# Split activations and weights in other places of SBUF: block pitches of 1040, 1056, 1072 and 2080 bytes in a hybrid mLSTM and gated-delta block

## The chip, the cores and the metric

The kernel runs on one core of one Trainium2 chip. The metric is the device time of one execution in microseconds (us); the time before is the median of three runs.

## What is computed

One layer of a bidirectional encoder block in float32, with 256 tokens of width 2048, and a final norm:

```python
mod = silu(c) @ W_ada + b_ada                    # shift, scale, gate for both sub-layers
h = rms_norm(x) * (1 + scale_m) + shift_m
proj = h @ w_in                                  # q, k, v, gates of two branches, merge gates
y_a = (sigmoid(a_o) * norm(bidirectional mLSTM)) @ w_branch_a
y_b = (norm(bidirectional gated delta rule) * silu(b_z)) @ w_branch_b
x = x + gate_m * ((g_a * y_a + g_b * y_b) @ w_out)
hf = rms_norm(x) * (1 + scale_f) + shift_f
gt, up = split(hf @ w_gate_up)                   # 2048 -> 2 x 5632
x = x + gate_f * ((silu(gt) * up) @ w_down)      # 5632 -> 2048
return rms_norm(x)
```

## The kernel before

Almost all of the work is large matrix products of the 256 tokens with weights that come once from HBM. For more precision than one pass of the fast float32 form (`float32r`) gives, each operand is split in a high part (a copy rounded to that form, made by ScalarE) and a low part (the remainder, a subtraction on VectorE). A product is then three matmuls: high x high, low x high, high x low.

The activations are kept split, transposed, in blocks of 128 features: a tile `[128, 16 blocks, 256 tokens]` of 16 KB in each partition, one for the high and one for the low part. `big` makes these for the mixer: `hh`/`hl` (the normed input), `obh`/`obl` and `hah`/`hal` (the outputs of the two branches), `mgh`/`mgl` (their merge). `hfh`/`hfl` (the normed input of the feed-forward part, 16 blocks) and `ffh`/`ffl` (its inner activation, 44 blocks) are made at their place (lines 876 to 879).

Weights are split as they arrive, in two kinds of job:

- `tjob` gives 256 tokens x 512 columns. A chunk of 1 MB (four blocks of 128 x 512) is loaded into `raw` by a DMA from the SP queue. For each pair of blocks ScalarE writes `wh` (line 153) and VectorE `wl` (line 154), and twelve matmuls follow: per block and token half the lines 159, 160 and 161. The **stationary** operand is a 128 x 128 piece of the activations, `xh` or `xl`; the **moving** one is a block of 512 columns of `wh` or `wl`. There are 32 such jobs of four chunks in the mixer (`z`, `v`, `o`, `ma`, `mb` on `hh`/`hl`, four each, `yb`, `ya` and the output projection, named `o` too in the profile, but with `mgh`/`mgl`), 22 in the feed-forward part (`gt`, `up`), and 4 of eleven chunks (`d`): 6240 matmuls.
- `fjob` gives 128 features x 256 tokens (names `b` and `a` in the profile, lines 135 to 137): there the weights are the stationary operand and `hh`/`hl` the moving one, with 256 columns. There are 49 such jobs: 2352 matmuls.

`raw`, `wh` and `wl` have three buffers each, which both kinds of job share; so each of `wh` and `wl` has three slots of 4 KB, and a slot holds two blocks of a `tjob`.

Until about 1175 us the jobs run as filling between the steps of the two recurrent branches and of the modulation vectors (`ada`, VectorE), in an order written out by hand. Then come `yb`, `ya`, the output projection, from about 1468 us on `gt` and `up` in turn, and from about 1966 us `d`, one job after the other.

The places of these tiles in a partition, before the change, in bytes:

| tile | start | modulo 128 | pitch of its blocks |
|---|---|---|---|
| `wh`, three slots | 46880, 50976, 55072 | 32 | 2048 (`tjob`), 512 (`fjob`) |
| `wl`, three slots | 59168, 63264, 67360 | 32 | 2048, 512 |
| `hh`, `hl` | 196576, 212960 | 96 | 1024 |
| `obh`, `obl` and later `mgl`, `mgh` | 79680, 96064 | 64 | 1024 |
| `hah`, `hal` | 196576, 212960 | 96 | 1024 |
| `hfh`, `hfl` | 169760, 186144 | 32 | 1024 |
| `ffh`, `ffl` | 71456, 116512 | 32 | 1024 |

The second half of the tokens lies 512 bytes behind the first, so it has the same remainder modulo 128.

Of the kernel before, what the change touches and what calls it, by code (L numbers as in the profile page):

```python
# [10 lines left out]
F32R = mybir.dt.float32r  # L11
# [4 lines left out]
P = 128  # L16
T = 256
D = 2048
KB = D // P
# [4 lines left out]
FB = FF // P  # L24
# [26 lines left out]
def hybrid_block(ctx: ExitStack, tc: tile.TileContext, xr, nfr, crow, pk_d, cst_d, ada2, ada4, win0, winb, wint, wba, wbb, wo, wgu, wd, out, dbg=None):  # L51
# [3 lines left out]
    def pool(stack, name, bufs=1, **kw):  # L55
        return stack.enter_context(tc.tile_pool(name=name, bufs=bufs, **kw))

    cp = pool(ctx, "cp")
    st = pool(ctx, "st")
# [4 lines left out]
    bigA = pool(sa, "bigA", 2, side="right")  # L64

    def big(p, dt, name):
        return p.tile([P, KB, T], dt, tag="b16", name=name)

    def gps(name):
        return g_ps.tile([P, 512], F32, tag="g", name=name)  # L70
# [45 lines left out]
    def pump():  # L116
        count[0] += 1
        if background and count[0] % 2 == 0:
            if next(background[0], None) is None:
                background.pop(0)  # L120
# [22 lines left out]
    def tjob(name, chunks, xh, xl, done):  # L143

        ps = [acc_ps.tile([P, 512], F32, tag="acc", name=f"acc_{name}_{t}") for t in range(2)]
        last = 4 * len(chunks) - 1
        for u, src in enumerate(chunks):
            raw = st.tile([P, 4, 512], F32, tag="raw", bufs=3, name=f"raw_{name}_{u}")
            nc.sync.dma_start(raw, src)
            for k0 in range(0, 4, 2):  # L150
                wh = st.tile([P, 2, 512], F32R, tag="wh", bufs=3, name=f"wh_{name}_{u}_{k0}")
                wl = st.tile([P, 2, 512], F32R, tag="wl", bufs=3, name=f"wl_{name}_{u}_{k0}")
                S.activation(wh, raw[:, k0 : k0 + 2], AF.Copy)  # L153
                V.tensor_tensor(wl, raw[:, k0 : k0 + 2], wh.bitcast(F32), ALU.subtract)  # L154
                for k in range(2):
                    kk = 4 * u + k0 + k
                    for t in range(2):
                        c = slice(t * P, (t + 1) * P)
                        PE.matmul(ps[t], xh[:, kk, c], wh[:, k], start=kk == 0, stop=False)  # L159
                        PE.matmul(ps[t], xl[:, kk, c], wh[:, k], start=False, stop=False)  # L160
                        PE.matmul(ps[t], xh[:, kk, c], wl[:, k], start=False, stop=kk == last)  # L161
                if k0:
                    pump()
                    if u == len(chunks) - 1:
                        done(ps)
                yield True
# [32 lines left out]
    inv_d = [tc.dram_tile([64, 32, 32], F32, name=f"inv_d{g}") for g in range(NH_B // GRP)]  # L199

    hh = big(bigA, F32R, "hh")
    hl = big(bigA, F32R, "hl")

    evp = pool(sa, "evp", side="right")
# [31 lines left out]
    with ExitStack() as s0:  # L236
# [24 lines left out]
        for b in range(KB):  # L261
# [6 lines left out]
            for i in range(2):  # L268
                f = 1.0 if i else pk[:, PK_NMIX + b : PK_NMIX + b + 1]
# [21 lines left out]
        u = w0.tile([P, T], F32, name="u")  # L291
# [275 lines left out]
    def z_job(g):  # L567
        def done(ps):
            szs[g] = evp.tile([P, 2, 512], F32, tag="sz", bufs=1, name=f"sz{g}")
            for t in range(2):  # L570
                S.activation(szs[g][:, t], ps[t], AF.Silu)
        return tjob(f"z{g}", [wint[g, u] for u in range(4)], hh, hl, done)
# [7 lines left out]
    def a_vo(i, h):  # L580
        return tjob(
            f"{'vo'[i]}{h}", [wint[4 + 4 * i + h, u] for u in range(4)], hh, hl,
            keep((v_d, o_d)[i][h], (AF.Copy, AF.Sigmoid)[i], f"{'vo'[i]}{h}"),
        )

    def m_job(i, g):
        return tjob(
            f"m{'ab'[i]}{g}", [wint[12 + 4 * i + g, u] for u in range(4)], hh, hl,
            keep((ma_d, mb_d)[i][g], AF.Sigmoid, f"m{'ab'[i]}{g}"),
        )  # L590
# [82 lines left out]
    bigC = pool(sc, "bigC", 2)  # L673
    ml = pool(sm_, "ml")
    obh, obl = big(bigC, F32R, "obh"), big(bigC, F32R, "obl")

    def o_split(g):
# [195 lines left out]
    fp = pool(ctx, "fp")  # L873
    sh = ExitStack()
    hp = pool(sh, "hp", side="right")
    hfh = hp.tile([P, KB, T], F32R, name="hfh")
    hfl = hp.tile([P, KB, T], F32R, name="hfl")
    ffh = fp.tile([P, FB, T], F32R, name="ffh")
    ffl = fp.tile([P, FB, T], F32R, name="ffl")
    for q in range(4):  # L880
        xn = hp.tile([P, 2, 512], F32, tag="sg", bufs=2, name=f"xn{q}")
        for t in range(2):
# [1 line left out]
        for e2 in range(2):  # L884
            px = gps(f"pxn{q}_{e2}")
            hf = hp.tile([P, 2, T], F32, tag="hf", bufs=1, name=f"hf{q}_{e2}")
            for e in range(2):
                f = 2 * e2 + e
# [14 lines left out]
    for j in range(FB // 4):  # L903
# [5 lines left out]
        for e2 in range(2):  # L909
            px = gps(f"pxf{j}_{e2}")  # L910
            for e in range(2):
                f = 2 * e2 + e
# [119 lines left out]
```

## Time and profile before

| | |
|---|---|
| median of 3 runs | 2219.57 us (2217.16 to 2230.97) |
| the profiled execution | 2226.21 us, span 2224.4 us |
| granted TensorE clock in it | 0.979 |
| TensorE busy | 2096.3 us (94%) |
| VectorE busy | 1408.9 us (63%) |
| ScalarE busy | 994.9 us (45%) |
| DMA | 485.83 MB, mean 218 GB/s |

PE is TensorE, PEld its loading of stationary operands, DVE is VectorE, ACT ScalarE, POOL GpSimd, SP SyncE. A group of instructions is shown by line, engine and operation, then out<-in by the names of the tiles with shapes and xcount; behind the first bar stand its busy time in us and the mean of one in ns, behind the second the engine's idle time before it and what ended that. A row of the timeline has its start in us, its length in us, engine, line, operation and tiles. A row of the windows has the stretch, its length, and for each engine its busy time with the number of its instructions; then the granted clock as a share, the share of DMA time and GB/s. Matmuls are pipelined and their ends are modelled, so their lengths overlap.

### The profile page before, as it was taken

The page shows a single profiled execution, that of the slowest core. Times are in us where ns is not written, and L with a number is a line of the kernel's source. Part 1 is how long each engine was busy: PE and PEld are TensorE (multiplying, and loading weights), DVE is VectorE, ACT ScalarE, POOL GpSimd, SP SyncE. Part 2 cuts the span into 40 slices and gives each one's busy share as a digit, 9 for nine tenths or more (in the row PEclk, how much of TensorE's full clock was granted, in tenths as well). Part 3 has the DMA queues.
Part 4 walks back from the last instruction along what each step waited for, and adds up shares of the span by engine and source line. Part 5 has one row for each costly group of instructions (what it writes and reads, how often), then busy time and mean ns, then how long its engine had stood idle before and what let it go on. Part 6 is the DMA issues. An engine that isn't in the chain of part 4 may idle for free.

```text
span 2224.4 us, 27756 instructions
## 1 busy us (share of the span) xinstructions
PE 2096.3 (94%) x10756; PEld 1754.7 (79%) x10756; DVE 1408.9 (63%) x2120; ACT 994.9 (45%) x1399; POOL 103.6 (5%) x206
## 2 busy tenths in 40 slices
PE   5989989998998899989999999989999999999997
PEld 4867778978887888778787787868888888878886
DVE  4677777886788677845557776564544454454454
ACT  3146436644564456434443444444444444444443
POOL 0002101100210111010000000000000000000000
PEclk9999999999999999999999999999999999999999
DMA  8976665675667455756787676545555555555553
GB/s 308 416 303 194 184 215 187 204 248 191 192 236 241 163 189 205 255 201 231 286 318 269 241 291 232 186 141 191 190 183 191 191 190 183 192 199 189 192 197 122
DMA packets 82645, 485.83 MB, mean 218 GB/s; under 512 B 10681, under 2 KB 21057, under 8 KB 28113
## 3 DMA queue, kind: packets, MB, share of 16 engines
q1 hardware_dynamic: 68672, 459.34, 58.0%
q0 software_dynamic: 6496, 9.49, 2.7%
q10 hardware_dynamic: 7346, 15.24, 1.8%
q8 instruction: 84, 1.38, 0.2%
q14 instruction: 47, 0.39, 0.0%
HBM read 467.21 MB, written 16.82 MB: 218 GB/s over the span
## 4 chain that ended last, share of the span: by engine, by line
PE 60%; DVE 4%; DMA 3%; issue 2%; ACT 1%; POOL 0%; DVEq 0%; ACTq 0%; POOLq 0%
PE acc_gt L159 4%; PE acc_gt L160 4%; PE acc_up L161 4%; PE acc_up L160 4%; PE acc_up L159 4%; PE acc_d L160 4%; PE acc_gt L161 4%; PE acc_d L159 4%; PE acc_d L161 4%; PE acc_o L160 2%; PE acc_o L161 2%; PE acc_o L159 2%; DMA ada<-ada 1%; PE acc_ya L160 1%; PE acc_ya L159 1%
## 5 line engine op out<-in xcount | busy, mean ns | idle before, releaser
L154 DVE TENSOR_TENSOR wl_up<-raw_up,wh_up 128x1024 fp32r<-128x1024 f32 x88 | 107.9, 1226 | 128.7 <-ACT wh_up L153 128.7
L154 DVE TENSOR_TENSOR wl_d<-raw_d,wh_d 128x1024 fp32r<-128x1024 f32 x88 | 107.8, 1226 | 123.2 <-ACT wh_d L153 123.2
L154 DVE TENSOR_TENSOR wl_gt<-raw_gt,wh_gt 128x1024 fp32r<-128x1024 f32 x88 | 107.8, 1225 | 109.3 <-ACT wh_gt L153 109.3
L107 DVE SCALAR_TENSOR_TENSOR ada<-ada,crow 128x2048 f32<-128x2048 f32 x64 | 146.2, 2284 | 39.2 <-DMA ada<-ada 39.2
L135 PE MATMUL acc_b<-hh,wh_b 128*128 128x256 f32 x576 | 167.3, 290 | 0.0
L137 PE MATMUL acc_b<-hh,wl_b 128*128 128x256 f32 x576 | 162.5, 282 | 1.1 <-DVE wl_b L132 1.1
L136 PE MATMUL acc_b<-hl,wh_b 128*128 128x256 f32 x576 | 162.9, 283 | 0.0
L153 ACT ACTIVATE wh_d<-raw_d 128x1024 fp32r<-128x1024 f32 x88 | 93.3, 1061 | 138.9 <-PE acc_d L160 132.0
L153 ACT ACTIVATE wh_gt<-raw_gt 128x1024 fp32r<-128x1024 f32 x88 | 93.3, 1060 | 133.9 <-PE acc_gt L160 78.9
L153 ACT ACTIVATE wh_up<-raw_up 128x1024 fp32r<-128x1024 f32 x88 | 93.2, 1060 | 117.8 <-PE acc_up L160 84.6
L159 PE MATMUL acc_gt<-wh_gt,hfh 128*128 128x512 f32 x352 | 138.8, 397 | 1.3 <-ACT hfh L183 1.1
L160 PE MATMUL acc_gt<-wh_gt,hfl 128*128 128x512 f32 x352 | 139.4, 396 | 0.0
L161 PE MATMUL acc_gt<-wl_gt,hfh 128*128 128x512 f32 x352 | 138.7, 394 | 0.0
L159 PE MATMUL acc_d<-wh_d,ffh 128*128 128x512 f32 x352 | 137.4, 390 | 0.0
L160 PE MATMUL acc_d<-wh_d,ffl 128*128 128x512 f32 x352 | 137.4, 390 | 0.0
L161 PE MATMUL acc_d<-wl_d,ffh 128*128 128x512 f32 x352 | 137.0, 389 | 0.0
L161 PE MATMUL acc_up<-wl_up,hfh 128*128 128x512 f32 x352 | 136.9, 389 | 0.0
L159 PE MATMUL acc_up<-wh_up,hfh 128*128 128x512 f32 x352 | 136.9, 389 | 0.0
L160 PE MATMUL acc_up<-wh_up,hfl 128*128 128x512 f32 x352 | 136.9, 389 | 0.0
L274 PE MATMUL first<-x,raw 128*128 128x256 f32 x512 | 111.6, 380 | 2.0 <-ACT x L271 2.0
L135 PEld LDWEIGHTS acc_b<-hh,wh_b 128*128 128x128 f32 x576 | 110.6, 192 | 2.1 <-issue 1.4
L137 PEld LDWEIGHTS acc_b<-hh,wl_b 128*128 128x128 f32 x576 | 110.8, 192 | 1.7 <-DVE wl_b L132 1.7
(339 smaller groups left out, 5375.8 us busy)
## 6 DMA issues: line engine op xcount, KB each, us to landing
ada<-ada SPq DMA_DIRECT2D x64, 1024.0 KB, 5.4
raw_gt<-wgu SPq DMA_DIRECT2D x44, 1024.0 KB, 4.9
raw_up<-wgu SPq DMA_DIRECT2D x44, 1024.0 KB, 4.9
raw_d<-wd SPq DMA_DIRECT2D x44, 1024.0 KB, 4.8
raw_b<-winb SPq DMA_DIRECT2D x36, 1024.0 KB, 5.4
ra<-ada SPq DMA_DIRECT2D x32, 1025.0 KB, 12.7
raw<-win SPq DMA_DIRECT2D x16, 1024.0 KB, 10.5
raw_z<-wint SPq DMA_DIRECT2D x16, 1024.0 KB, 5.8
```

The lines of the kernel that those rows point to most:

```text
L107: V.scalar_tensor_tensor(raw, raw, 1.0, row_c[:, :D], ALU.mult, ALU.mult, accum_out=mod[:, c0 + b : c0 + b + 1])
L135: PE.matmul(o, wh[:, k], hh[:, kk], start=kk == 0, stop=False)
L136: PE.matmul(o, wh[:, k], hl[:, kk], start=False, stop=False)
L137: PE.matmul(o, wl[:, k], hh[:, kk], start=False, stop=kk == KB - 1)
L153: S.activation(wh, raw[:, k0 : k0 + 2], AF.Copy)
L154: V.tensor_tensor(wl, raw[:, k0 : k0 + 2], wh.bitcast(F32), ALU.subtract)
L159: PE.matmul(ps[t], xh[:, kk, c], wh[:, k], start=kk == 0, stop=False)
L160: PE.matmul(ps[t], xl[:, kk, c], wh[:, k], start=False, stop=False)
L161: PE.matmul(ps[t], xh[:, kk, c], wl[:, k], start=False, stop=kk == last)
L274: PE.matmul(first[o], raw[:, o], x[:, b], start=b == 0 and o % 2 == 0, stop=b == KB - 1 and o % 2 == 1)
```

## The change

The tiles that hold split operands are made a little longer in their last dimension, and only the old part of each is used. `big` allocates 260 instead of 256 tokens (16 bytes more a block, 16640 instead of 16384 bytes a tile), `wh` and `wl` of `tjob` 520 instead of 512 columns (32 bytes; the slots, which `fjob` shares, grow from 4096 to 4160 bytes), `hfh`/`hfl` 264 tokens (32 bytes), `ffh`/`ffl` 268 tokens (48 bytes). Everything allocated behind them moves by the difference: on the left side by 6 x 64 = 384 bytes, on the right by 512. Order, engines, operations and shapes of the instructions stay as they are; operands that spread over several blocks have a step between the blocks.

```diff
     def big(p, dt, name):
-        return p.tile([P, KB, T], dt, tag="b16", name=name)
+        return p.tile([P, KB, T + 4], dt, tag="b16", name=name)[:, :, :T]
...
             for k0 in range(0, 4, 2):
-                wh = st.tile([P, 2, 512], F32R, tag="wh", bufs=3, name=f"wh_{name}_{u}_{k0}")
-                wl = st.tile([P, 2, 512], F32R, tag="wl", bufs=3, name=f"wl_{name}_{u}_{k0}")
+                wh = st.tile([P, 2, 520], F32R, tag="wh", bufs=3, name=f"wh_{name}_{u}_{k0}")[:, :, :512]
+                wl = st.tile([P, 2, 520], F32R, tag="wl", bufs=3, name=f"wl_{name}_{u}_{k0}")[:, :, :512]
...
-    hfh = hp.tile([P, KB, T], F32R, name="hfh")
-    hfl = hp.tile([P, KB, T], F32R, name="hfl")
-    ffh = fp.tile([P, FB, T], F32R, name="ffh")
-    ffl = fp.tile([P, FB, T], F32R, name="ffl")
+    hfh = hp.tile([P, KB, T + 8], F32R, name="hfh")[:, :, :T]
+    hfl = hp.tile([P, KB, T + 8], F32R, name="hfl")[:, :, :T]
+    ffh = fp.tile([P, FB, T + 12], F32R, name="ffh")[:, :, :T]
+    ffl = fp.tile([P, FB, T + 12], F32R, name="ffl")[:, :, :T]
```

## The prediction

> **What bounds the kernel now.** I read the page's engine totals first, then three windows of the span, then the groups of the last stage.
>
> ```profile
> PE 2096.3 (94%) x10756; PEld 1754.7 (79%) x10756; DVE 1408.9 (63%) x2120; ACT 994.9 (45%) x1399; POOL 103.6 (5%) x206
> ...
> PE 60%; DVE 4%; DMA 3%; issue 2%; ACT 1%; POOL 0%; DVEq 0%; ACTq 0%; POOLq 0%
> ...
> L154 DVE TENSOR_TENSOR wl_d<-raw_d,wh_d 128x1024 fp32r<-128x1024 f32 x88 | 107.8, 1226 | 123.2 <-ACT wh_d L153 123.2
> ...
> L153 ACT ACTIVATE wh_d<-raw_d 128x1024 fp32r<-128x1024 f32 x88 | 93.3, 1061 | 138.9 <-PE acc_d L160 132.0
> ...
> L159 PE MATMUL acc_d<-wh_d,ffh 128*128 128x512 f32 x352 | 137.4, 390 | 0.0
> ```
>
> ```profile
> core 0: us, PE busy (x) PEld busy (x) DVE busy (x) ACT busy (x) POOL busy (x), PEclk, DMA share, GB/s
> 0.00:1175.00 1175.00, 1068.44 (x6222) 921.20 (x6222) 833.73 (x1513) 558.01 (x909) 103.63 (x206) 0.97 0.68 236
> 1175.00:1460.00 285.00, 283.62 (x1235) 225.30 (x1236) 188.44 (x222) 119.86 (x148) 0.00 (x0) 0.99 0.68 243
> 1460.00:2225.00 765.00, 744.24 (x3301) 608.24 (x3299) 386.73 (x387) 317.08 (x342) 0.00 (x0) 0.99 0.54 182
> ```
>
> TensorE has work in 94% of the span. Behind 1175 us it hardly stops: ScalarE waits for TensorE (L153 <-PE), VectorE for ScalarE, TensorE for nobody (0.0 idle before L159). There a split pair costs ScalarE 1.061 and VectorE 1.226 us, while its 12 matmuls take 12 x 0.2267 = 2.72 us, so both have slack. The 390 ns "mean" of a matmul is a modelled length that overlaps the next one. What counts is the distance from start to start, which I take from the timeline: first and last row of a stretch without a gap, over the number of steps between.
>
> In the d stage (stationary ffh/ffl, both 32 past a multiple of 128, as the moving wh/wl are), 178 rows:
>
> ```profile
> 1999.82 0.39 PE L160 MATMUL acc_d<-wh_d,ffl 128*128 128x512 f32 x1
> ...
> 2039.94 0.39 PE L160 MATMUL acc_d<-wh_d,ffl 128*128 128x512 f32 x1
> ```
>
> 40.12 / 177 = 0.2267 us. In the o stage (stationary mgh/mgl, 64 past a multiple of 128), 173 rows:
>
> ```profile
> 1399.72 0.40 PE L161 MATMUL acc_o<-wl_o,mgh 128*128 128x512 f32 x1
> ...
> 1439.85 0.40 PE L159 MATMUL acc_o<-wh_o,mgh 128*128 128x512 f32 x1
> ```
>
> 40.13 / 172 = 0.2333 us. The windows of both (us, TensorE busy and its matmuls, granted clock, DMA share, GB/s) show a full clock:
>
> ```profile
> 1400.00:1440.00 40.00, 40.00 (x173) 1.00 0.56 188
> 1980.00:2200.00 220.00, 220.00 (x973) 1.00 0.55 186
> ```
>
> The instructions have the same line and shape; what differs is where the stationary blocks lie. With hh/hl (96 past a multiple of 128) there are two values, over 37 and 36 rows:
>
> ```profile
> 249.71 0.39 PE L161 MATMUL acc_v<-wl_v,hh 128*128 128x512 f32 x1
> ...
> 257.95 0.39 PE L161 MATMUL acc_v<-wl_v,hh 128*128 128x512 f32 x1
> ...
> 689.71 0.40 PE L160 MATMUL acc_z<-wh_z,hl 128*128 128x512 f32 x1
> ...
> 697.88 0.40 PE L159 MATMUL acc_o<-wh_o,hh 128*128 128x512 f32 x1
> ```
>
> 8.24 / 36 = 0.2289 and 8.17 / 35 = 0.2334 us: the same places give either, so the rhythm locks into one of several states. How it settles is to be seen in the feed-forward stage behind a break:
>
> ```profile
> 1522.21 0.39 PE L160 MATMUL acc_gt<-wh_gt,hfl 128*128 128x512 f32 x1
> 1522.44 0.40 PE L161 MATMUL acc_gt<-wl_gt,hfh 128*128 128x512 f32 x1
> 1522.67 0.39 PE L159 MATMUL acc_gt<-wh_gt,hfh 128*128 128x512 f32 x1
> 1522.90 0.40 PE L160 MATMUL acc_gt<-wh_gt,hfl 128*128 128x512 f32 x1
> 1523.13 0.39 PE L161 MATMUL acc_gt<-wl_gt,hfh 128*128 128x512 f32 x1
> 1523.37 0.39 PE L159 MATMUL acc_gt<-wh_gt,hfh 128*128 128x512 f32 x1
> ```
>
> Five steps take 1.16 us, 0.232 each, before it falls to 0.2267. So a rhythm that isn't locked costs about 0.232, and the best lock is that of places with equal remainders, which is what the feed-forward stages have.
>
> At half clock the excess is gone. The window 685 to 688 us, then its first and last of eight rows:
>
> ```profile
> 685.00:688.00 3.00, 3.00 (x8) 0.50 0.49 126
> ...
> 685.05 0.63 PE L160 MATMUL acc_z<-wh_z,hl 128*128 128x512 f32 x1
> ...
> 688.04 0.63 PE L161 MATMUL acc_z<-wl_z,hh 128*128 128x512 f32 x1
> ```
>
> 2.99 / 7 = 0.427, half of which is 0.2136: the floor that a full-clock matmul would have without the excess of 0.013 to 0.020 us.
>
> **The change part by part.** No instruction is added, removed or moved. The start of every block of the split operands changes, and the 6240 matmuls of 512 columns read both operands from them. Pitches become 1040 bytes for hh/hl and all other 16-block activations, 1056 for hfh/hfl, 1072 for ffh/ffl, 2080 between the two halves of wh/wl. Modulo 128 the moving operand then begins at 32 or 96 (first half) and at 0 or 64 (second half); the stationary one steps by 16, 32 or 48 from block to block. The equal remainders of the feed-forward stages are given up: this is the change's cost.
>
> (1) gt and up, 2112 matmuls. The stationary blocks step by 32, so differences from the moving operand are multiples of 32. The rows give 0.2267 for 0, 0.2289 for 64, 0.2333 for 32 (64 against 32); I take 0.2333 for 96 too, mean 0.2306. 2112 x 0.0039 = +8.2 us. Bounds: 0, if each matmul finds the best lock, and 2112 x 0.0066 = +13.9, if each has the worst.
>
> (2) d, 1056 matmuls, steps of 48, each pair with another difference: I take the unlocked 0.232, +5.6 us; bounds 0 and +7.0.
>
> (3) Jobs on hh/hl (z, v, o, ma, mb), 1920 matmuls, steps of 16: now between 0.2289 and 0.2334, middle 0.2312; afterwards 0.232: +1.5 us, bounds -8.6 (all at 0.2267) and +8.4 (0.2289 to 0.2333).
>
> (4) ya, 384 matmuls, whose hah/hal lie as hh/hl do, from 0.2289: +1.2 us. yb and the output projection, 768, from 0.2333: -1.0. Together between -5.9 and +1.7.
>
> (5) The feature-major jobs, 2352 matmuls of 256 columns. Here hh is the moving operand. Two rhythms, 18 and 15 rows:
>
> ```profile
> 835.95 0.28 PE L137 MATMUL acc_b<-hh,wl_b 128*128 128x256 f32 x1
> ...
> 837.88 0.28 PE L136 MATMUL acc_b<-hl,wh_b 128*128 128x256 f32 x1
> ...
> 832.94 0.28 PE L136 MATMUL acc_b<-hl,wh_b 128*128 128x256 f32 x1
> ...
> 834.59 0.28 PE L135 MATMUL acc_b<-hh,wh_b 128*128 128x256 f32 x1
> ```
>
> 1.93 / 17 = 0.1135 and 1.65 / 14 = 0.1179. Both states are there already; I take 0, bounds -5 and +5 (half the difference x 2352).
>
> (6) ScalarE and VectorE write wh, wl and the split activations in pieces with a gap between. Places off a multiple of 16 bytes are read already: the convolution's four taps begin 0, 4, 12 and 16 bytes into a padded row.
>
> ```profile
> L233 DVE SCALAR_TENSOR_TENSOR cv<-pad,pk,cv x192: 440/479/490, 146.7 to 874.1; 128x256 f32<-128x256 f32 x192
> ```
>
> Minimum, median and maximum over the 192 lie within 50 ns, so a start costs VectorE next to nothing. I take 0. If each split grew by 50 ns, the 2.29 us of a pair stay below 2.72 and are hidden behind the matmuls. Without that cover, in the first 1175 us, the 274 splits there (20 jobs of 8, 49 of 2, 16 blocks of hh) x 0.05 = +14 us at worst.
>
> Sum: 8.2 + 5.6 + 1.5 + 1.2 - 1.0 = +15.5 us. The profiled execution took 2226.2 (span 2224.4 and 1.8 around it), so it would come to 2241.7; it lies 6.6 above the median shown, 2219.6, and against that median the forecast is 2235.
>
> **The rivals.**
>
> Faster: the excess over 0.2136 comes from a start that is off by 32 modulo 64. Every moving block that the rows show begins so, and none of these matmuls reaches the floor; that speaks for it as far as it goes. Afterwards the second halves of wh/wl begin at multiples of 64. If these 3120 matmuls fall from 0.2267 to 0.2136, that is -41 us, and the other half pays half of my sum, +8: 2187. Against it: only the stationary place differs between 0.2267 and 0.2333, so the excess is at least partly a meeting of the two reads.
>
> Slower still: differences of an odd multiple of 16, which no row shows, cost a further step as large as from 0.2267 to 0.2333, so 0.24. This touches half of d and half of the jobs on hh, ya, yb and o: 2064 x 0.008 = 16.5. The 1176 feature-major matmuls with such a moving block pay 0.0066 as well, 7.8. With my sum, +40: 2260. For it: each smaller unit of misplacement in the rows (64, then 32) costs more. Against it: 32 against 64 could be the worst case.
>
> No change: the difference between the stages has another cause than the remainders, or blocks that begin at multiples of 16 are all alike. Then 2220. By the Trainium skill, SBUF — State Buffer, section "Specifications (TRN2)", a line is 16 bytes long, and by its "Who interferes with whom" TensorE's two read ports are independent and TensorE waits for no one; all starts here stay on such lines, so by that rule the change moves nothing. The rows of one line and shape at 0.2267 and 0.2333 speak against that reading of the rule. Nor does the kernel become another program: VectorE, ScalarE and the queues keep order and sizes.
>
> **How the numbers follow.** The places in steps (1) and (2) leave a lock that only equal remainders show, and I see no way to keep it: 50 in 100 for the forecast, 2235 with its own range 2222 to 2252. Faster 22 in 100 (2187), slower still 18 (2260), no change 10 (2220). A measurement of this kernel can tell about 1% from no change, 22 us: 2197 and 2242. Of the forecast's 50, 20 lie beyond 2242, since the bounds of (1) to (4) add up to +31. So faster by over 1% is 0.22, within 1% 0.30 + 0.10 = 0.40, slower 0.20 + 0.18 = 0.38. The range goes from 2184, just below the faster case, to 2268, just above the slower one; about one in ten is left out on each side.
>
> **What would show it.** If right, the d stage's rows are no longer 0.2267 apart but spread over 0.226 to 0.24 with a mean near 0.232, the o stage's come down slightly from 0.2333, the last window grows by some 14 us and the first hardly, and the splits keep 1.06 and 1.23 us. Steps of about 0.214 to 0.22 behind every second half of wh/wl would show the faster rival; a mean of 0.24 in d beside 0.231 in gt and up, the slower one. Longer splits at L153 and L154 with TensorE waiting for them would make the whole argument wrong, since it is about TensorE's reads alone.

## The result, and the profile after

The changed kernel takes 2244.35 us (median of 9 runs, 2237.08 to 2258.57) against 2224.89 us of the kernel before on the same chip (9 runs, 2217.16 to 2233.02). The ratio, which is close to the quotient of the two medians but not the same, is 1.0092 with a 95% interval of 1.007 to 1.0115: the change costs about 20 us (15.6 to 25.6), a loss of just under 1% that is clear of the scatter. The profiled execution took 2252.85 us (span 2251.1).

The page of the changed kernel (engine totals, chain by engine, groups of the last stage):

```profile
PE 2131.7 (95%) x10756; PEld 1772.2 (79%) x10756; DVE 1409.8 (63%) x2120; ACT 995.5 (44%) x1399; POOL 103.6 (5%) x206
...
L154 DVE TENSOR_TENSOR wl_d<-raw_d,wh_d 128x1024 fp32r<-128x1024 f32 x88 | 107.8, 1225 | 128.2 <-ACT wh_d L153 128.2
...
L153 ACT ACTIVATE wh_d<-raw_d 128x1024 fp32r<-128x1024 f32 x88 | 93.4, 1061 | 144.0 <-PE acc_d L160 136.9
...
L159 PE MATMUL acc_d<-wh_d,ffh 128*128 128x512 f32 x352 | 139.0, 395 | 0.0
```

Only TensorE's busy times changed clearly: 2131.7 against 2096.3 us for the matmuls. A part of this may be the lower granted clock of this execution (0.974 against 0.979). The splits in pieces cost what they did, 1.061 and 1.225 us. ScalarE waits longer for TensorE (136.9 against 132.0), and TensorE still waits for nobody in `d`. So TensorE is slower with the same work, not stopped by something new.

Rows of its timeline: first and last of a gap-free stretch of `b` (47 rows), the first rows of `gt` behind two successive breaks, and the `d` stage (519 rows, of which the first, the last, and a few in between):

```profile
821.89 0.28 PE L136 MATMUL acc_b<-hl,wh_b 128*128 128x256 f32 x1
...
827.34 0.28 PE L137 MATMUL acc_b<-hh,wl_b 128*128 128x256 f32 x1
...
1580.43 0.39 PE L160 MATMUL acc_gt<-wh_gt,hfl 128*128 128x512 f32 x1
...
1625.82 0.40 PE L160 MATMUL acc_gt<-wh_gt,hfl 128*128 128x512 f32 x1
...
2009.74 0.39 PE L159 MATMUL acc_d<-wh_d,ffh 128*128 128x512 f32 x1
...
2058.87 0.39 PE L161 MATMUL acc_d<-wl_d,ffh 128*128 128x512 f32 x1
2059.10 0.40 PE L159 MATMUL acc_d<-wh_d,ffh 128*128 128x512 f32 x1
2059.34 0.40 PE L160 MATMUL acc_d<-wh_d,ffl 128*128 128x512 f32 x1
2059.57 0.39 PE L161 MATMUL acc_d<-wl_d,ffh 128*128 128x512 f32 x1
...
2129.80 0.39 PE L161 MATMUL acc_d<-wl_d,ffh 128*128 128x512 f32 x1
```

and the same `b` stretch and the same point of `gt` in the kernel before:

```profile
819.35 0.28 PE L136 MATMUL acc_b<-hl,wh_b 128*128 128x256 f32 x1
...
824.58 0.28 PE L137 MATMUL acc_b<-hh,wl_b 128*128 128x256 f32 x1
...
1566.76 0.39 PE L160 MATMUL acc_gt<-wh_gt,hfl 128*128 128x512 f32 x1
...
1611.29 0.39 PE L160 MATMUL acc_gt<-wh_gt,hfl 128*128 128x512 f32 x1
```

In `d` 120.06 / 518 = 0.2318 us a step, against 0.2267; by the packed trace, which has starts to the nanosecond, single steps lie between 0.224 and 0.241. Two successive `gt` jobs, with the `up` job between them, start 45.39 us apart, against 44.53: a **pair** of jobs has 192 matmuls, so each costs 0.0045 us more (the small matmuls in the break between two jobs are in both). This distance from pair to pair is the ruler of the sections below: it needs no count of rows. A step of `b` takes 5.45 / 46 = 0.1185 us against 5.23 / 46 = 0.1137.

The mean distance from start to start over all matmuls of a kind (from each trace; only steps below 0.245 us, for the 256 columns of `b` and `a` below 0.150, so that waits are left out), in ns; `o` is given apart for hh and for mg:

| kernel | z, v, ma, mb, o (hh) | yb | ya | o (mg) | gt, up | d | b, a |
|---|---|---|---|---|---|---|---|
| before | 229.3 to 230.4 | 233.2 | 229.0 | 233.3 | 227.2, 226.7 | 226.7 | 114.5 |
| after | 231.9 to 232.2 | 231.9 | 232.0 | 231.9 | 231.4, 231.5 | 231.8 | 118.2 |

By these the feed-forward stages cost 1056 x (4.2 + 4.8 + 5.1) ns = 14.9 us more; ya, yb and the output projection together 0.1; the jobs before them 4.6 (hh) and 8.7 (feature-major), if nothing hid any of it. That is 28 us of TensorE time, where 20 arrive.

### The profile page after: what moved, and what is told of

Same layout as the page of the kernel before. It is cut to its first block, busy times and chain, and to the rows that moved or that the text cites. A ratio compares the mean times of both kernels' runs of the same rounds, so it can differ in the third digit from the quotient of the medians.

```text
span 2251.1 us, 27756 instructions
## 1 busy us (share of the span) xinstructions
PE 2131.7 (95%) x10756; PEld 1772.2 (79%) x10756; DVE 1409.8 (63%) x2120; ACT 995.5 (44%) x1399; POOL 103.6 (5%) x206
## 4 chain that ended last, share of the span: by engine, by line
PE 61%; DVE 3%; DMA 3%; issue 2%; ACT 0%; POOL 0%; DVEq 0%; ACTq 0%; POOLq 0%
PE acc_gt L159 4%; PE acc_gt L160 4%; PE acc_up L161 4%; PE acc_up L160 4%; PE acc_d L160 4%; PE acc_d L161 4%; PE acc_d L159 4%; PE acc_gt L161 4%; PE acc_up L159 4%; PE acc_o L160 2%; PE acc_o L161 2%; PE acc_o L159 2%; PE acc_ya L160 1%; PE acc_ya L161 1%; PE acc_ya L159 1%
## 5 line engine op out<-in xcount | busy, mean ns | idle before, releaser
L153 ACT ACTIVATE wh_d<-raw_d 128x1024 fp32r<-128x1024 f32 x88 | 93.4, 1061 | 144.0 <-PE acc_d L160 136.9
```

## The experiments

**Theory:** the cost of a matmul hangs on the *relation*, the start of its stationary block less the start of its moving block; equal remainders are best, and the change gives them up. **Rivals:** the place of one operand alone decides; the pitch of the blocks in itself decides; or something in the mixer's order pays.

**One part of the change at a time.** First the feed-forward activations alone (`ffn_only`):

```diff
-    hfh = hp.tile([P, KB, T], F32R, name="hfh")
+    hfh = hp.tile([P, KB, T + 8], F32R, name="hfh")[:, :, :T]
     # hfl alike; ffh, ffl with T + 12
```

> Only hfh/hfl (pitch 1056) and ffh/ffl (pitch 1072) are moved; wh/wl and the mixer's tiles stay. Theory 1 (relation): what counts is how the start of the moving block stands to the start of the stationary block, modulo 128, and that this no longer repeats. gt, up and d go from 0.2267 to about 0.2315 us a matmul (3168 x 0.0048 = +15 us, ratio 1.007); the window up to 1460 us stays. Theory 2 (the moving start alone): the moving blocks still all begin 32 past a multiple of 128, so 0.2267 stays and the ratio is 1.000. Theory 3 (sum of parts): the three parts done alone add up to the whole, +19.5 us; this one is then at most what the other two leave.

Then the mixer's activations alone (`mixer_only`, `T + 4` in `big`), and the weights alone (`weights_only`, 520 columns for `wh` and `wl` in `tjob`):

> Only the tiles of big (hh, hl, obh, obl, hah, hal, mgh, mgl, pitch 1040) are moved. Theory 1: the feed-forward stages stay at 0.2267; the jobs z, v, o, ma, mb go from 0.2297 to about 0.232 (+4.5 us), ya from 0.229 to 0.232 (+1.2), yb and the output projection from 0.2333 to 0.232 (-1.0), the feature-major jobs from 0.1145 to 0.118 (2352 x 0.0037 = +8.7 us, as in the changed kernel, since hh is what they stream): +13 us, ratio 1.006. Theory 2: z, v, o, ma, mb, ya, yb keep their times to 0.0003 (moving starts unchanged), only the feature-major jobs change: +9 us. If wh/wl is what slowed the feature-major jobs, these stay at 0.1145.

> Only wh and wl of the 512-column jobs are moved (halves 2080 bytes apart, slots 4160), so the moving block begins 32, 96, 0 or 64 past a multiple of 128; every stationary block keeps its remainder. Theory 1: the relation changes from matmul to matmul in all stages: gt, up, d at about 0.2315 (+15 us), z, v, o, ma, mb, ya near 0.232 (+5.5), yb and the output projection near 0.232 (-1): +19 us, ratio 1.009, although two of three parts are undone; parts then add up to far more than the whole (15 + 13 + 19 against 19.5). Theory 2: the second halves, which begin at 0 or 64 past a multiple of 128, are dearer by the same amount in all stages, and the first halves stay. Theory 3: what ffn_only and mixer_only leave of 19.5 us.

| kernel | median, before beside it (us) | ratio, 95% | z to o (hh) | yb, ya, o (mg) | gt, up, d | b, a |
|---|---|---|---|---|---|---|
| ffn_only | 2244.09, 2225.91 | 1.0079 (1.0054 to 1.0104) | 229.2 | 233.2, 229.0, 233.3 | 232.7, 232.6, 231.8 | 114.5 |
| mixer_only | 2227.31, 2225.91 | 0.9998 (0.9976 to 1.0019) | 231.6 | 231.2, 231.6, 231.2 | 227.2, 226.7, 226.7 | 118.1 |
| weights_only | 2242.67, 2225.91 | 1.0064 (1.0042 to 1.0086) | 231.5 | 231.4, 231.1, 231.3 | 232.0, 231.8, 230.9 | 117.6 |

Timeline rows: `gt` from break to break in ffn_only,

```profile
1573.81 0.39 PE L160 MATMUL acc_gt<-wh_gt,hfl 128*128 128x512 f32 x1
...
1619.44 0.39 PE L160 MATMUL acc_gt<-wh_gt,hfl 128*128 128x512 f32 x1
```

in weights_only,

```profile
1575.01 0.39 PE L160 MATMUL acc_gt<-wh_gt,hfl 128*128 128x512 f32 x1
...
1620.49 0.39 PE L160 MATMUL acc_gt<-wh_gt,hfl 128*128 128x512 f32 x1
```

and in mixer_only `b` (47 rows) and `d` (178 rows):

```profile
817.88 0.28 PE L136 MATMUL acc_b<-hl,wh_b 128*128 128x256 f32 x1
...
823.32 0.28 PE L137 MATMUL acc_b<-hh,wl_b 128*128 128x256 f32 x1
...
2019.67 0.39 PE L160 MATMUL acc_d<-wh_d,ffl 128*128 128x512 f32 x1
...
2059.79 0.39 PE L160 MATMUL acc_d<-wh_d,ffl 128*128 128x512 f32 x1
```

A pair takes 45.63 us in ffn_only, where only the stationary side was moved, and 45.48 in weights_only, where only the moving side was; before it was 44.53. By the distances ffn_only should cost 1056 x (5.5 + 5.9 + 5.1) ns = 17.4 us, and 0.0079 x 2226 = 17.6 were measured; weights_only 14.9 (gt, up, d), measured 14.2. The stage itself shows the same: from the first start of `gt` to the last of `d` the profiled executions took 740.6 us before, 754.9 in the changed kernel, 756.9 in ffn_only, 755.1 in weights_only and 740.5 in mixer_only. So the loss sits in the feed-forward stages, and since moving either operand alone brings it, the place of one operand alone doesn't decide. The parts do not add up (18 and 14 against 20 together), as is to be expected if it is the relation: either side alone breaks it. mixer_only slowed its matmuls as forecast (`b` 5.44 / 46 = 0.1183, `d` unchanged 40.12 / 177 = 0.2267), but the forecast of a longer time missed: no change, though yb and o with 2 ns less and ya with 2.6 more nearly cancel. What TensorE loses ahead of `yb` hardly reaches the end here.

**Each job at its own offset** (`scan`): every job's `wh` and `wl` lie some multiple of 4 bytes further, in slots of 4224 bytes.

```diff
-                wh = st.tile([P, 2, 512], F32R, tag="wh", bufs=3, ...)
+                wh = st.tile([P, 1056], F32R, tag="wh", bufs=3, ...)
+                wh = wh[:, off : off + 1024].rearrange("p (k c) -> p k c", k=2)   # wl alike
```

> All stationary blocks keep their remainders modulo 128; each job writes its wh and wl at an offset of its own (0 to 30 elements of 4 bytes into slots of 4224 bytes), the same within the job. So each of the 58 jobs of 512 columns and 49 of 256 columns has one relation throughout. Theory 1: within a job the rhythm locks; each relation modulo 128 has its own value: 0.2267 at offset 0 in gt, up and d (equal remainders), 0.233 at 32 bytes, 0.229 or 0.2333 at 64 bytes, and yb and the output projection (stationary 64) reach 0.2267 at an offset of 32 bytes, the jobs on hh and ya (stationary 96) at 64 bytes. Offsets of an odd multiple of 16 and of single elements are open: between 0.2267 and 0.236. Theory 2: the value depends on the offset alone, whatever the stationary remainder is, and an offset of 32 bytes (moving start a multiple of 64) might go down to 0.214 to 0.220 in every stage.

The first `d` job has offset 0, so its places are equal to the stationary ones modulo 128. The timeline, first and last of its 241 rows:

```profile
1979.34 0.39 PE L182 MATMUL acc_d<-wl_d,ffh 128*128 128x512 f32 x1
...
2034.96 0.39 PE L182 MATMUL acc_d<-wl_d,ffh 128*128 128x512 f32 x1
```

55.62 / 240 = 0.2318, not 0.2267. The slots are now 33 x 128 bytes apart, so they differ by 128 modulo 256. The remainder modulo 128, on which the whole prediction was built, is not enough. The sweep was meant as a map; with that flaw it is none. (The time of its one run, 2234.55 us, means little.)

**Equal remainders everywhere, and alignment.** In `equal` each activation tile is 512 bytes longer, and its blocks begin so far in that all stationary blocks have the remainder of the moving ones modulo 512:

```diff
+OFF = {'hh': 80, 'hl': 80, 'obh': 120, ..., 'hfh': 0, 'hfl': 0, 'ffh': 0, 'ffl': 0}    # in columns of 4 bytes
-        return p.tile([P, KB, T], dt, tag="b16", name=name)
+        t = p.tile([P, KB * T + 128], dt, tag="b16", name=name)
+        return t[:, OFF[name] : OFF[name] + KB * T].rearrange("p (k t) -> p k t", k=KB)
```

`on_512` does the same with all starts, moving and stationary, at multiples of 512 bytes: the rival of the prediction that a start off by 32 modulo 64 causes the excess.

> Pitches of whole KB as in the kernel before, but every stationary tile begins at the remainder modulo 512 that the moving blocks have (288), as ffh/ffl and hfh/hfl do already. Theory 1 (a relation that repeats from matmul to matmul locks the rhythm; equal remainders give the best lock): all 512-column matmuls at 0.2267; z, v, o, ma, mb from 0.2296, ya from 0.229, yb and the output projection from 0.2333. Behind 1160 us that saves 768 x 0.0066 + 384 x 0.0023 = 6 us; before it 1920 x 0.0029 = 5.6 us at most, which waits hide. Ratio 0.997 (0.995 to 0.998). Theory 2 (the moving start alone): nothing changes, 1.000. A theory that only the pitch counts (whole KB or not): 1.000 too.

> As equal, but wh, wl and all stationary tiles begin at multiples of 512 bytes (everything 224 bytes further on the left). Theory 1: only the relation counts, so again 0.2267 in all stages, ratio 0.997. Theory 2 (a start off by 32 modulo 64 is what costs 0.011 us above the half-clock floor of 0.2136): 0.214 to 0.220 in all stages, 6240 x 0.007 to 0.012, of which behind 1160 us 4300 x 0.01 = -43 us: ratio 0.98.

Timeline of equal, `b` and `yb` (47 rows each):

```profile
823.28 0.28 PE L139 MATMUL acc_b<-hl,wh_b 128*128 128x256 f32 x1
...
828.79 0.28 PE L140 MATMUL acc_b<-hh,wl_b 128*128 128x256 f32 x1
...
1217.87 0.39 PE L163 MATMUL acc_yb<-wh_yb,obl 128*128 128x512 f32 x1
...
1228.30 0.40 PE L164 MATMUL acc_yb<-wl_yb,obh 128*128 128x512 f32 x1
```

and of on_512, `d` (179 rows):

```profile
2039.64 0.39 PE L163 MATMUL acc_d<-wh_d,ffl 128*128 128x512 f32 x1
...
2079.98 0.39 PE L164 MATMUL acc_d<-wl_d,ffh 128*128 128x512 f32 x1
```

`yb` falls from 0.233 to 10.43 / 46 = 0.2267; all jobs of 512 columns now have means of 226.7 to 227.8. But `b` rises to 5.51 / 46 = 0.1198 (mean 119.8): for the feature-major jobs equal places are the worst seen. The time is 2227.89 us against 2226.81, ratio 0.9999 (0.9979 to 1.0019): the expected gain of 0.3% didn't come. The dearer `b` and `a`, 2352 x 5.3 ns = 12.5 us of TensorE time, may have eaten it; that is argued, not shown. on_512 measured 40.34 / 178 = 0.2266 and 1.0005 (0.9988 to 1.0022): alignment in itself brings nothing, and the rival with 0.2136 falls. Its expected 0.997 missed too.

**Fixed relations, one for each stage.** The same edit as in equal with other offsets. `relations` sets 256 (hh), 128 (ob), 384 (ha), 64 (mg), 16 (hf) and 48 (ff) bytes. `unequal_parts` sets only the low parts apart (hfl 256, ffl 128, obl 64, hal 32, mgl 16), which asks whether the relation of two stationary blocks in succession counts too.

> Whole KB pitches; each stage has one fixed relation, stationary start minus moving start modulo 512: hh/hl 256, obh/obl 128, hah/hal 384, mgh/mgl 64, hfh/hfl 16, ffh/ffl 48. Theory 1: each stage locks into a repeating pattern of one to three distances (few values in the histogram), at a mean of its own between 0.2267 and 0.2335; if the relation counts modulo 128 only, then z, v, o, ma, mb, yb and ya all show 0.2267. A theory in which 16-byte steps are dear by themselves: gt and up at 0.232 or more, d too. In the scan with changing relations 16 was the cheapest on average (0.2286); if that carries over, gt and up come below 0.2286.

> Whole KB pitches; the high stationary tiles have the moving blocks' remainder (288 modulo 512), the low ones stand off it: hfl by 256, ffl by 128, obl by 64, hal by 32, mgl by 16 bytes. So line 160 has one relation, lines 159 and 161 another, in the same order all the time. Theory 1 with locking by repetition: a pattern that repeats every three matmuls can lock too, and the mean stays at 0.2267 where the difference is a whole period of the memory's order (256 or 128, if that is the period), and goes to 0.228 to 0.233 for 64, 32, 16. In the scan the slots differed by 128 bytes and no job with offset 0 was at 0.2267 (0.2318, 0.2323): if 128 is what unlocked it, d is at 0.229 to 0.232 here, else at 0.2267.

Timeline of relations, `z` (39 rows) and `gt` from break to break:

```profile
693.66 0.39 PE L162 MATMUL acc_z<-wh_z,hh 128*128 128x512 f32 x1
...
702.30 0.39 PE L164 MATMUL acc_z<-wl_z,hh 128*128 128x512 f32 x1
...
1577.39 0.40 PE L163 MATMUL acc_gt<-wh_gt,hfl 128*128 128x512 f32 x1
...
1623.15 0.40 PE L163 MATMUL acc_gt<-wh_gt,hfl 128*128 128x512 f32 x1
```

A relation of 256 is as good as 0 (8.64 / 38 = 0.2274), while 128 and 384 give means of 232.6 and 232.4. So the **period is 256 bytes**. With 16 bytes a pair takes 45.76 us, more than in the changed kernel. The profiled execution, the only one, took 2253.31 us. In unequal_parts (2230.76 us, one execution) hfl at 256 bytes leaves `gt` and `up` at 227.1 and 226.7; ffl at 128 gives `d` 231.1, obl at 64 gives `yb` 231.2 and hal at 32 gives `ya` 233.2, though two thirds of the matmuls keep equal places. Yet mgl at 16 leaves `o` at 226.8, and that I can't explain: how strongly one third of the matmuls pulls the rest along is open.

**Is it the pitch?** `pitch_1280` gives hfh/hfl a pitch of 1280 bytes, which is no whole number of KB but leaves every relation at 0 modulo 256. `relations_2` and `relations_3` fill the map: 128, 240, 224, 96, 208, 160 and 64, 80, 144, 176, 4, 8 bytes for hh, ob, ha, mg, hf, ff.

```diff
-    hfh = hp.tile([P, KB, T], F32R, name="hfh")
+    hfh = hp.tile([P, KB, T + 64], F32R, name="hfh")[:, :, :T]      # hfl alike
```

> The kernel before with hfh/hfl alone at a pitch of 1280 bytes, that is 256 bytes of room behind each block: the pitch is no longer whole KB, but every block keeps its remainder modulo 256 (32, as the moving blocks). Theory 1 with a period of 256 bytes: gt and up stay at 0.2267. If it is the whole KB that counts (or the gap between the blocks), they go to 0.2315 to 0.2327 as in ffn_only. If the period is 512, they go to about 0.23, since the remainder alternates.

> Whole KB pitches, one fixed relation (stationary minus moving start modulo 256) for each stage: hh/hl 128, obh/obl 240, hah/hal 224, mgh/mgl 96, hfh/hfl 208, ffh/ffl 160. Theory 1: each locks into a few distances with a mean between 0.2267 and 0.2335, none as low as 0.2267, since only 0 (and 256) was; hh/hl at 128 as yb with 128: 0.2326. A rival in which some other relation avoids the meeting altogether shows 0.214 to 0.222 in one of them; that would be worth 1 to 2% of the time.

> The same with hh/hl 64, obh/obl 80, hah/hal 144, mgh/mgl 176, hfh/hfl 4, ffh/ffl 8 bytes: the remaining multiples of 16 and two offsets below 16. Theory 1: hh/hl 64 as the output projection had it with 64 (0.2333); 80, 144, 176 between 0.229 and 0.2335; 4 and 8 break the 16-byte alignment of the stationary blocks as well: in the scan, moving starts 4 off cost 0.236, 8 off 0.233. The same rival: one of them at 0.214 to 0.222.

Timeline of pitch_1280, `gt` from break to break, and of relations_2, the `o` stage (286 rows):

```profile
1565.73 0.39 PE L160 MATMUL acc_gt<-wh_gt,hfl 128*128 128x512 f32 x1
...
1610.28 0.39 PE L160 MATMUL acc_gt<-wh_gt,hfl 128*128 128x512 f32 x1
```

```profile
1399.72 0.40 PE L164 MATMUL acc_o<-wl_o,mgh 128*128 128x512 f32 x1
...
1466.50 0.39 PE L164 MATMUL acc_o<-wl_o,mgh 128*128 128x512 f32 x1
```

In pitch_1280 a pair takes 44.55 us, as before: a pitch that is no whole number of KB costs nothing as long as the remainder modulo 256 stays. The one execution of it took 2225.11 us; those of relations_2 and relations_3 took 2248.6 and 2245.95. A relation of 96 costs 66.78 / 285 = 0.2343, the most of any. The map so far, mean distance in ns of matmuls of 512 columns by relation modulo 256:

| bytes | 0 | 16 | 32 | 48 | 64 | 80 | 96 | 128 | 144 | 160 | 176 | 192 | 208 | 224 | 240 |
|---|---|---|---|---|---|---|---|---|---|---|---|---|---|---|---|
| ns | 226.7 | 232.7 | 233.2 | 233.3 | 233.3 | 232.1 | 234.2 | 232.5 | 233.3 | 233.3 | 230.0 | 229 or 233.4 | 232.1 | 233.3 | 227.9 |

The values at 0, 32 and 192 are those of the kernel before: hf and ff have 0, ob and mg 32, hh and ha 192. In relations_3 4 bytes give 232.4 and 8 bytes 230.7; 112 was not tried. No relation comes near 0.214 to 0.222, so the rival of these expectations falls. Of the fifteen in the row 0 is the cheapest, and 240 is close behind: 227.9 in `yb`, which at relation 0 (in equal) took 227.3. The feed-forward stages had 0.

The map holds for a relation that stays. What happens when it changes is in the trace of ffn_only. There all moving blocks begin 32 past a multiple of 256 and the blocks of hfh/hfl step by 32 bytes, so that six matmuls in succession have one relation. In `up` the mean step is 231.1 ns for relation 0 and 230.4 for 192, and 232.8 to 233.8 for the other six. In `d`, where the relation changes after one or two matmuls, the sixteen means lie between 230.1 and 234.0, relation 0 at 231.1, and not in the order of the map (96 at 231.0, 240 at 234.0). So equal places are cheap where they **repeat**, and a run of six matmuls is too short for it; the unchanged `gt`, too, has five uneven steps behind the break shown in the prediction before it settles at 226 and 227. The mean of the row (192 taken as 229.5) is 231.8, and the stages of the changed kernel lie at 231.4 to 232.2; by these steps that agreement doesn't mean that each matmul pays the price of its own relation.

**Only the late mixer stages equal** (`late_equal`: as equal, but hh where it was, so that the feature-major jobs keep their state). If the map is right this should beat both the kernel before and equal.

> As equal, but hh/hl keep the relation they have in the kernel before (192 modulo 256 as stationary), which the feature-major jobs like (0.1135 or 0.118, against 0.1197 with equal remainders); only obh/obl, hah/hal, mgh/mgl get the moving blocks' remainder. Theory 1: yb and the output projection 0.2333 to 0.2267, ya 0.229 to 0.2267: 768 x 0.0066 + 384 x 0.0023 = -6 us behind 1160 us, and nothing lost before: ratio 0.997 (0.995 to 0.999). If the relation's gain is hidden by other waits there too, 1.000.

2222.17 us against 2224.52, ratio 0.9989 (0.997 to 1.0009). The distances came out as meant (yb 227.4, ya 227.1, o 226.9, `b` and `a` 114.9 and 114.4), which is worth 384 x (5.8 + 1.9 + 6.4) ns = 5.4 us. A gain of that size fits in the interval, but it isn't clear of none.

**Where the rest of the 20 us comes from.** The feed-forward stages explain 15, and the feature-major jobs are the largest other term. `feature_jobs_only` puts only `fjob`'s `wh` 192 bytes further, and leaves all else at its place:

```diff
-            wh = st.tile([P, 8, P], F32R, tag="wh", bufs=3, name=f"wh_{name}_{k0}")
+            wh = st.tile([P, 1088], F32R, tag="wh", bufs=3, name=f"wh_{name}_{k0}")
+            wh = wh[:, 48:1072].rearrange("p (k c) -> p k c", k=8)
```

> The kernel before; only wh of the feature-major jobs begins 192 bytes later in its slot (slots of wh 4352 bytes), so that it has hh's remainder modulo 256 (224), while wl keeps its relation and all 512-column jobs keep theirs. By the map of relations these 2352 matmuls go from 0.1145 to about 0.118 (two of three loads at the costly relation 0): +8 us of TensorE. If this reaches the end, as the later start of yb in the profiles of the slowed kernels suggests (about 1168 against 1161 us), the ratio is 1.003 (0.002 to 0.004). If the waits of the first 1160 us hide it, as the ratio 0.9998 of mixer_only suggests, 1.000.

`b` and `a` went to 118.0 and 117.9, all other kinds stayed. That is 2352 x 3.5 ns = 8 us more for TensorE, and the time became 2229.1 against 2225.17 us, ratio 1.0009 (0.9989 to 1.0029): by the interval at most 6.5 us of the 8 arrive. How far the kernels have come by 1160 us, where `yb` starts, is in the windows (first 1160 us: TensorE, its weight loads, VectorE, ScalarE and GpSimd with their counts, the granted clock, DMA share, GB/s); of before, of after, of mixer_only and of feature_jobs_only:

```profile
0.00:1160.00 1160.00, 1055.79 (x6171) 911.89 (x6172) 821.62 (x1493) 551.26 (x898) 103.63 (x206) 0.97 0.67 236
```

```profile
0.00:1160.00 1160.00, 1063.96 (x6130) 920.01 (x6131) 814.15 (x1486) 545.96 (x892) 103.59 (x206) 0.96 0.66 233
```

```profile
0.00:1160.00 1160.00, 1062.71 (x6170) 916.62 (x6171) 821.62 (x1493) 551.28 (x898) 103.55 (x206) 0.97 0.68 236
```

```profile
0.00:1160.00 1160.00, 1059.68 (x6115) 919.67 (x6116) 812.73 (x1485) 545.00 (x891) 103.34 (x206) 0.96 0.67 231
```

The stretch has some 100 us in which TensorE waits. In mixer_only its slower matmuls are taken from these: 7 us more busy, and 6170 matmuls done against 6171. In the changed kernel 41 matmuls are missing, in feature_jobs_only 56, at a granted clock of 0.96 instead of 0.97. As mixer_only slows the same jobs as much, this difference is not the slower matmuls alone. Single executions don't size a term of some us: ffn_only, which changes nothing ahead of `gt`, starts `yb` at 1165.0 us against 1160.2 before (1171.1 in the changed kernel). And weights_only, with the same loss in the feed-forward stages and nearly the same slower jobs ahead of them, came to 14.2 us in all (9.3 to 19.1), of which these jobs need have no part.

## Why the prediction was right or wrong

The sum was near: +15.5 forecast, +19.5 between the medians, and its mechanism, matmuls that lose equal places, is shown by ffn_only, weights_only, equal and pitch_1280. What failed is the step from the sum to the call, and three terms of the sum were too small: (5), (3) and (1). Most of the profile moved as said under "What would show it": `d` at 0.2318 with single steps from 0.224 to 0.241, `o` down from 233.3 to 231.9, splits unchanged, the feed-forward stages 14.4 us longer. That the first window would hardly grow is not seen in the profiled execution, in which `yb` starts 11 us later. Point by point:

- **The call itself failed.** "Within 1%" was given the largest chance, because I took 1% for what a measurement can tell. The comparison told 0.23% to either side, so a loss of 0.92% is a clear loss. My own sum was a loss of 0.7%, and the range that I gave it, 2222 to 2252, lay wholly above the time before; read against the resolution reached, it said slower. (That range doesn't follow from the terms, whose lower bounds for (1) to (4) add up to -14.5 us.)
- **Step (1), gt and up**, was too small: +8.2 with a mean of 0.2306; measured 0.2314 and 0.2315, +9.5. The step averaged four relations modulo 128 and gave a quarter of the matmuls the low price of 0.2267. Scan and relations show that the period is 256, so that equal places come half as often; and in ffn_only they don't get the low price even where six matmuls in a row have them (0.2311).
- **Step (2), d**: +5.6 with 0.232; measured 0.2318, +5.4. Right, and the reason given, that no relation lasts, fits the steps of ffn_only. That five uneven steps behind a break had the mean of a whole stage was in part luck.
- **Step (3), jobs on hh**, was too small: +1.5, since I set the old state at 0.2312 from two rhythms taken half and half. Its mean was 0.2297, so +4.6 of TensorE time. mixer_only shows that hardly anything of it reaches the end.
- **Step (4)**: ya +1.2, yb and output projection -1.0; measured +1.2 and -1.0. Right.
- **Step (5), feature-major jobs**, was mis-sized at 0: 0.1145 became 0.1182, +8.7 us of TensorE time, beyond the bound of 5. The two rhythms of the rows were taken as an even mixture that stays. In `b` three quarters of the steps before were of the faster one (0.113 to 0.115); in the changed kernel the steps spread from 0.112 to 0.125 around 0.118. feature_jobs_only leaves at most 6.5 us of it in the time.
- **Step (6), splits**: 0, and 1.061 and 1.225 us are as before. Right.

So (1) was short by 1.3, and the two terms that were set far too low, (3) and (5), by 11.8 us of TensorE time together, lie where TensorE also waits: that the sum still came near is in part luck. At +15.5 it stands just below the interval of the result, 15.6 to 25.6.

Of the rivals, "faster" falls with on_512: starts on multiples of 512 keep 0.2267, and no step of the changed kernel's `d` is shorter than 0.224. "Slower still" has a grain of truth in 0.2343 at a relation of 96, but the odd multiples of 16 are no worse than the even ones (16 gives 232.7 and 32 gives 233.2). "No change" falls with ffn_only.

What stays open: which of the jobs ahead of 1160 us bring the remaining some 5 us of the 20 (the interval reaches from 1 to 11), or whether they bring any, since weights_only showed no clear loss beyond its feed-forward stages; why the relation 192 and the feature-major jobs have two states; and by what mechanism matmuls at starts equal modulo 256 bytes settle in a cheap rhythm.

## What to carry to other kernels

Where TensorE runs without a break, read the distance from start to start of matmuls of one shape stage by stage: a difference between stages with the same instruction points to the places of its operands. In this kernel 512 columns of float32r with a weight load each cost 0.2267 us when both operands start equal modulo 256 bytes for many matmuls in a row, and 0.228 to 0.234 at the other relations tried; block pitches that are multiples of 256 bytes keep such a relation, padding by 16 to 48 bytes destroys it. Price it only where TensorE is the bound: of 13 us of slower matmuls ahead of `yb` a part at most arrived, while the 15 us behind it arrived.

## What the runs showed of the hardware that was not expected

The period of 256 bytes (256 as good as 0, 128 and 384 at 232.5), and that it is the relation and not the place (0.2266 on multiples of 512 as at 32 past a multiple of 128). By the Trainium skill, SBUF — State Buffer, section "Who interferes with whom", TensorE has one read port for the moving operand and an independent one for weight loads. The trace does not agree with independence in time: ffn_only moved nothing but the blocks that the weight loads read, and the matmuls of `gt` and `up` went from about 0.227 to 0.2327 and 0.2326.

For 256 columns, where the weights are the stationary operand, the order is turned round: of the four relations seen (start of the weights less that of hh, modulo 256) equal places cost most, 119.8 ns, 128 cost 118.8 (relations_2), 192 cost 117.7 (relations_3), and 64, that of the kernel before, 114.5 on average, in rhythms of 113.5 and 117.9. The best place for one kind of job on a shared tile is thus the worst for the other, and equal gained nothing.
